# Gated output weights and the context's initial states made during the in-projection and kept in scratch memory

## The chip, the cores and the metric

The kernel runs on one core of one Trainium2 chip. TensorE (PE) multiplies matrices, VectorE (DVE), ScalarE (ACT) and GpSimd (POOL) do the rest, SyncE (SP) issues most transfers. Each engine takes its instructions strictly in the order in which the program lists them. The metric is the device time in microseconds; three runs of the kernel before took 2037.56, 2040.84 and 2042.3 us, median 2040.84.

## The reference

One block of a network over 2048 tokens of width 1024 and 256 context tokens: normalise and modulate, project (`w_in`), mix the tokens by windowed attention and by a gated linear recurrence (mLSTM) run in both directions, project with `w_out`, then 16 experts of which each takes 256 tokens. What bears on the change, cut from the reference:

```
hx = modulate(rmsnorm(x, norm1_w), sh1, sc1);  hc = the same of ctx
aq, ak, av, mq, mk, mv, mo, gates = mixer_inputs(hx, ...)       # and of hc
att  = latent_attention(rope(aq), rope(ak), av, cak, cav, sink)
# DEPTH is 1, so the context only gives the recurrence its two initial states:
st_f = mlstm_state_update(zero, cmk, cmv, cli_f, clf_f)          # C = sum_s ws[s] k[s] v[s]
st_b = mlstm_state_update(zero, flip(cmk), flip(cmv), ...)
h_sum, _, _ = bidir_mlstm(mq, mk, mv, li_f, lf_f, li_b, lf_b, st_f, st_b)   # 16 chunks of 128, each way
mix  = concat([att, rmsnorm_per_head(h_sum) * norm_w * sigmoid(mo)])
x    = x + g1 * (mix @ w_out)                                    # g1: 1024 gates, the same for all tokens
x    = x + g2 * expert_choice_ffn(modulate(rmsnorm(x, norm2_w), sh2, sc2), ...)
```

All is float32. The kernel multiplies float32 matrices by splitting each operand into a rounded part (`hi`) and the rest (`lo`) and adding the products hi*hi, lo*hi and hi*lo.

## The kernel before, in words

**The planner.** Work is written as generators that yield what they need: an engine and a cost (`A(n)` ACT, `V(n)` DVE, `G(n)` POOL, `"P"` PE, `Q(n)` transfers), a token of a buffer pool, or an event. `Flow.run` (L108 on) plays these against a list of clocks, takes on each engine the ready task with the lowest priority number, and so fixes the order of instructions on each engine when the program is built. On the chip that order is kept, and an instruction waits for its operands and for the memory that it overwrites. `Flow(AHEAD)` lets the transfer queue of a phase begin AHEAD us before the phase's other engines.

**phase_in** (L427). `main` (L781) runs over four blocks of 512 tokens and, within a block, over eleven groups of columns of `w_in` (the last ones `mk`, `mv`, `mo`); the products land in the two PSUM buffers `mm`. `conv_out` (L835) empties those of `mq` and `mk` into a buffer `cu` (4 of them), convolves, and stores to `s_mq`, `s_mk`, `s_cmk`; `mo_out` (L906) stores `s_mo`. Attention runs beside it: scores (L258, L262), softmax, transposes of the probabilities (L303), values (L331, L332). `load_x` brings tokens through the buffers `xt` (3) and `hxv` (2). `mod_rest` (L1094) uses the same `xt` for the rest of the modulation weights, in 64 pieces multiplied and added on DVE into `macc`; it writes the gates g1 to `s_row`. `gates` (L1185) makes the recurrence's decay weights in block 3, among them `cws`, the context's.

**phase_mix** (L1365) has 32 visits, alternately the next chunk of the forward and of the backward direction. A visit loads query and key (`raw`, L1650) and value (`vraw`, L1664), makes the weights `wh`, `wl` (`prep_s`, `prep_w`) and the decayed query (`prep_q`, `decb`), gives its output with L1912 and updates the state `C` with L1624; the split state is `cs`. The second visit of a chunk adds both directions, normalises and, in `out_proj` (L2075), multiplies by `w_out` rows 512 to 1023 (weights 4 to 7) and makes router logits. `att_loads`, `att_projs` (L2008, L2034) multiply the attention's part by weights 0 to 3, one chunk after another beside the first visits; the second visits' loads wait until these are done.

The parts that the change touches: `inits` (L1520) loads the context's `cmv` and `cmk`, splits the values into `vsl` (2 buffers), transposes the keys, scales them by `cws` and makes both initial states and their splits. `wouts` and `wout` (L1469, L1498) load g1 and `w_out`, multiply (L1503; L1506 also by the norm's weights), and split into `wo_hi` and `wo_lo` (four pairs, of 128 by 1024; weights 4 to 7 take the same four pairs after the last attention projection). `prep_k` waits for `got_ev`, which `inits` fires late. The first loads' buffers (`raw`, `vraw`, `decb`, `xl`, `hx2t`) lie in one pool on the right side of the memory, where phase_in has `hxp`:

Of the kernel before, what the change touches and what calls it, by code (L numbers as in the profile page):

```python
# [16 lines left out]
try:  # L17
# [15 lines left out]
D = 1024  # L33
# [18 lines left out]
PRI = dict(loadx=1, mod1=0, hx=10, w=5, main=11, sc=6, tr=6, val=8, modr=11, gates=1, norm=6, rows=0, hxsp=3, hx0=1, wsp=0, conv=6, kv=7, q=6, mv=5, mo=5, rq=8, rk=3, value=1, ml=4, mrl=8, sm=10, usp=11, st=11)  # L52
# [3 lines left out]
AHEAD = 5.0  # L56
RIGHT = ("raw", "vraw", "decb", "xl", "hx2t")
# [5 lines left out]
PR = dict(vs=12, masks=7, init=0, load=8, vload=13, wout=6, dir=10, wr=2, hload=11, xload=0, pw=6, pq=5, ps=2, ks=7, se=10, h=2, he=7, xe=2, sc=12, ce=10, wout2=1, pk=13, asp=7, ae=10, ap=13, fi=4, op=13, aload=13, lo=13, af=6)  # L63
# [19 lines left out]
    "row": (2, 1024),  # L83
}
# [23 lines left out]
class Flow:  # L108
# [37 lines left out]
    def follow(self):  # L146
        self.cur.ready -= self.lag["D"]

# [208 lines left out]
class Kernel:  # L357
# [69 lines left out]
    def phase_in(self):  # L427
        nc, tc = self.nc, self.tc
        with ExitStack() as st:
# [26 lines left out]
            self.mod_ev, self.opened, self.main_done, self.rest_ev, self.turned = (Event() for _ in range(5))  # L456
# [21 lines left out]
            fl.spawn(self.gates(), PRI["gates"])  # L478
            fl.run()
# [6 lines left out]
    def load_x(self, units):  # L486
        nc, a, p, tok = self.nc, self.a, self.hxp, self.tok
        for n, u in enumerate(units):
# [4 lines left out]
            for t in range(2):  # L493
                if n < 2:
                    yield self.wm_ev[XW_AT[n]]
                if n < 2:
                    x = (self.ep if n else self.mp).tile([128, D], F32, name=f"xe{t}")
                else:
                    yield tok["xt"]
                    x = self.buf(p, "xt", [128, D])  # L500
# [10 lines left out]
    def norm_x(self, x, ev):  # L511
        nc, p, tok = self.nc, self.hxp, self.tok
        yield tok["hxv"]
        junk = self.buf(p, "hxv", [128, D], BF)
# [391 lines left out]
    def mo_out(self, ps, i, u, t):  # L906
# [17 lines left out]
        (nc.scalar if u == ("x", 7) else nc.sync).dma_start(self.s["mo"][r0:r0 + 128, i * 256:(i + 1) * 256], e)  # L924
# [260 lines left out]
    def gates(self):  # L1185
# [36 lines left out]
        for ct in range(2):  # L1222
# [13 lines left out]
            self.fl.give(mm)  # L1236
        yield mm
# [113 lines left out]

    def logsig_flow(self, x):
# [12 lines left out]
    def phase_mix(self):  # L1365
        nc, tc, a, s = self.nc, self.tc, self.a, self.s
        self.rk = self.last.enter_context(tc.tile_pool(name="rkeep", bufs=1, reuse_waits="tile"))
        with ExitStack() as st:
# [5 lines left out]
            right = pool("pmixr", 1, side="right", reuse_waits="tile")  # L1374
            self.alt = dict.fromkeys(RIGHT, right)
            fl = self.fl = Flow(AHEAD)
            self.bufs = MBUFS
            self.tok = {n: Tokens(k, -AHEAD if n in RIGHT else 0.0) for n, k in MBUFS.items()}
# [5 lines left out]
            self.wo_ev, self.stored, self.wr_ev, self.init_ev = evs(8), evs(NT), Event(), evs(2)  # L1384
            self.got_ev = Event()
            self.mask_ev, self.att_ev, self.wf_ev = Event(), Event(), evs(2)
# [53 lines left out]
    def wrouter(self):  # L1440
        nc, a, one, tok = self.nc, self.a, self.one_p, self.tok
        self.wr = one.tile([128, KT, NE], F32, name="wr")
        yield Q(128)
# [25 lines left out]
    def wouts(self):  # L1469
        nc, a, s, tok, fl = self.nc, self.a, self.s, self.tok, self.fl  # L1470
        yield tok["hx2t"]
        g1b = self.buf(self.pin, "hx2t", [128, 1024])
        yield Q(1024)
        nc.sync.dma_start(g1b, self.dram(s["row"], 0, [[0, 128], [1, 1024]]))
        left = [8]
        for k in range(4):
            yield tok["xl"]
            wf = self.buf(self.pin, "xl", [128, 1024])
            if k == 3:
                fl.fire(self.wf_ev[0])  # L1480
            yield Q(1024)
            nc.sync.dma_start(wf[0:64, :], a["w_out"][k * 64:(k + 1) * 64, :])
            nc.sync.dma_start(wf[64:128, :], a["w_out"][256 + k * 64:256 + (k + 1) * 64, :])
            fl.spawn(self.wout(k, wf, g1b, "xl", left), PR["wout"])
        yield self.s_ev[NT // 2]
        for k in range(4, 8):
            buf = "xn" if k < 6 else "xl"
            if k == 6:
                yield self.am_ev[NT - 1]
            yield tok[buf]  # L1490
            wf = self.buf(self.pin, buf, [128, 1024])
            if k == 7:
                fl.fire(self.wf_ev[1])
# [1331 lines left out]
```

## Time and profile before

| What | Value |
|---|---|
| median of three runs | 2040.84 us |
| the profiled execution | 2042.06 us, of which the span of the trace is 2040.3 |
| busy over the span | PE 1863.0 us (91%), DVE 1595.5 (78%), ACT 1280.7 (63%), POOL 839.1 (41%) |
| instructions | 37000 |
| read and written in HBM | 270.73 MB and 84.54 MB, 174 GB/s over the span |
| mean granted TensorE clock | 0.959 of full speed |

All later numbers of the trace are microseconds from the span's start. "Busy" adds the durations of an engine's instructions; an engine may be busy all the time and still not decide the end, since others may wait for something else. DMA share is the mean busy share of the 16 DMA engines. "[idle before <-X]" behind an instruction says how long its engine stood before it and what ended that.

### The profile page before, as it was taken

The numbers are of one execution on the slowest core, as the hardware profiler recorded it, in microseconds if no ns is written. First come the engines' busy times: TensorE is split into PE (matmuls) and PEld (weight loads), VectorE is DVE, ScalarE is ACT, GpSimd is POOL, SyncE is SP. The second block draws the span as 40 slices with busy tenths as digits, with TensorE's granted clock in tenths as the row PEclk, the third lists the DMA queues.
The fourth block names the chain that finished last, engine by engine and source line by source line (L and its number), as shares of the span: only waits on it lengthen the run. The fifth ranks groups of instructions, "written<-read, shape, count | busy, mean of one in ns | idle before, by whom it ended". The sixth has DMA issues, their size and how long they took to land.

```text
span 2040.3 us, 37000 instructions
## 1 busy us (share of the span) xinstructions
PE 1863.0 (91%) x12921; PEld 1665.6 (82%) x12921; DVE 1595.5 (78%) x3486; ACT 1280.7 (63%) x3144; POOL 839.1 (41%) x820
## 2 busy tenths in 40 slices
PE   7799999999999999996989989994589999999997
PEld 2698998899889989985767767783589999999996
DVE  3799779998998699868999677756667878787772
ACT  4477777787787777775665578865344545454542
POOL 0324234333543243316777665510334535353432
PEclk9899999999999999996999989996699999999999
DMA  8343264345342333227777867646467878888772
GB/s 281 98 145 102 73 189 123 109 149 160 99 120 79 95 84 97 79 82 205 270 255 260 286 224 242 225 145 222 133 203 210 261 226 253 240 235 254 223 233 42
DMA packets 293499, 357.82 MB, mean 175 GB/s; under 512 B 27288, under 2 KB 225592, under 8 KB 292416
## 3 DMA queue, kind: packets, MB, share of 16 engines
q1 hardware_dynamic: 283072, 320.32, 49.9%
q0 software_dynamic: 9376, 34.08, 7.2%
q8 instruction: 102, 1.67, 0.3%
q10 hardware_dynamic: 864, 1.05, 0.1%
q14 instruction: 85, 0.70, 0.1%
HBM read 270.73 MB, written 84.54 MB: 174 GB/s over the span
## 4 chain that ended last, share of the span: by engine, by line
PE 56%; DVE 24%; ACT 8%; DMA 6%; issue 5%; SPq 1%; POOL 0%; POOLq 0%; DVEq 0%; ACTq 0%
PE gu L2684 17%; PE mm L758 9%; PE yp L2736 8%; PE po L2004 5%; DVE w_lo L741 3%; PE t L303 2%; DMA w_raw<-in_w_in 2%; PE s L258 2%; PE o L593 1%; PE t L2628 1%; PE h L1912 1%; PE o L332 1%; PE o L331 1%; PE mm L776 1%; DVE s L280 1%
## 5 line engine op out<-in xcount | busy, mean ns | idle before, releaser
L2529 ACT ACTIVATE ew_hi<-ew_raw 128x1024 fp32r<-128x1024 f32 x184 | 193.6, 1056 | 163.6 <-PE yp L2736 91.5
L2457 DVE TENSOR_TENSOR ew_lo<-ew_raw,ew_hi 128x1024 fp32r<-128x1024 f32 x152 | 215.6, 1428 | 42.0 <-ACT ew_hi L2529 21.4
L291 POOL TENSOR_SCALAR P<-P,am 128x640 f32<-128x640 f32 (+1 forms) x128 | 113.1, 885 | 257.7 <-DVE am L289 145.4
L741 DVE TENSOR_TENSOR w_lo<-w_raw,w_hi 128x256 fp32r<-128x256 f32 (+1 forms) x352 | 157.3, 471 | 30.2 <-ACT w_hi L735 28.1
L2756 POOL DMA_INDIRECT out_x<-y,idx x32 | 57.1, 1786 | 260.7 <-DVE y L2750 175.0
L2684 PE MATMUL gu<-xg_hi,ew_hi 128*128 128x256 f32 x1024 | 148.6, 283 | 0.6 <-DVE xg_hi L2656 0.6
L758 PE MATMUL mm<-w_hi,hx_hi 128*128 128x256 f32 (+1 forms) x944 | 142.5, 288 | 5.2 <-ACT hxr L933 2.2
L735 ACT ACTIVATE w_hi<-w_raw 128x256 fp32r<-128x256 f32 (+1 forms) x352 | 135.2, 410 | 18.9 <-DMA w_raw<-in_w_in 18.1
L758 PE MATMUL mm<-w_hi,hx_lo 128*128 128x256 f32 (+1 forms) x944 | 141.9, 288 | 0.0
L2684 PE MATMUL gu<-xg_lo,ew_hi 128*128 128x256 f32 x1024 | 141.7, 280 | 0.0
L758 PE MATMUL mm<-w_lo,hx_hi 128*128 128x256 f32 (+1 forms) x944 | 141.5, 286 | 0.0
L2684 PE MATMUL gu<-xg_hi,ew_lo 128*128 128x256 f32 x1024 | 141.2, 280 | 0.0
L758 PEld LDWEIGHTS mm<-w_hi,hx_hi 128*128 128x128 f32 x944 | 124.8, 190 | 9.4 <-issue 2.7
L2684 PEld LDWEIGHTS gu<-xg_hi,ew_hi 128*128 128x128 f32 x1024 | 131.2, 189 | 1.0 <-DVE xg_hi L2656 0.9
L2684 PEld LDWEIGHTS gu<-xg_lo,ew_hi 128*128 128x128 f32 x1024 | 129.2, 189 | 0.0
L2684 PEld LDWEIGHTS gu<-xg_hi,ew_lo 128*128 128x128 f32 x1024 | 128.8, 189 | 0.0
L758 PEld LDWEIGHTS mm<-w_hi,hx_lo 128*128 128x128 f32 x944 | 125.0, 191 | 3.3 <-issue 2.6
L758 PEld LDWEIGHTS mm<-w_lo,hx_hi 128*128 128x128 f32 x944 | 124.6, 189 | 1.8 <-issue 0.9
L314 DVE TENSOR_TENSOR pl<-t,ph 128x512 fp32r<-128x512 f32 x156 | 105.8, 684 | 24.4 <-ACT ph L312 23.1
L282 ACT ACTIVATE P<-s,am 128x640 f32<-128x640 f32 (+1 forms) x128 | 99.8, 780 | 31.1 <-DVE am L280 25.7
L2750 DVE SCALAR_TENSOR_TENSOR y<-yp,gv,g2b 128x512 f32<-128x512 f32 x64 | 48.1, 751 | 90.2 <-PE yp L2736 90.2
L280 DVE CUSTOM_DVE_ANT_0 s<-s,mrow,nsink 128x640 f32<-128x640 f32 (+1 forms) x120 | 105.3, 877 | 13.1 <-PE s L262 7.5
(482 smaller groups left out, 5616.4 us busy)
## 6 DMA issues: line engine op xcount, KB each, us to landing
w_raw<-in_w_in SPq DMA_DIRECT2D x176, 256.0 KB
ew_raw<-in_w_gate SPq DMA_DIRECT2D x32, 1024.0 KB
ew_raw<-in_w_up SPq DMA_DIRECT2D x32, 1024.0 KB
ew_raw<-in_w_down SPq DMA_DIRECT2D x32, 1024.0 KB
xt<-in_w_mod SPq DMA_DIRECT2D x64, 256.0 KB
out_x<-xl SPq DMA_DIRECT2D x32, 512.0 KB
s_vs<-vsl SPq DMA_DIRECT2D x16, 516.0 KB
vsl<-s_vs SPq DMA_DIRECT2D x16, 516.0 KB
```

Source lines behind the costliest of these rows:

```text
L280: nc.vector.tensor_tensor_reduce(x, x, mask, 1.0, k.nsink[:, h:h + 1], op0=OP.add, op1=OP.min, accum_out=m[:, 0:1])
L282: nc.scalar.activation(P[:, :n], sc, AF.Exp, bias=m[:, 0:1], scale=-1.0, accum_out=m[:, 1:2])
L291: nc.gpsimd.tensor_scalar(P[:, :n], P[:, :n], m[:, 4:5], 0.0, op0=OP.mult, op1=OP.add)
L314: nc.vector.tensor_sub(lo, pt, f(hi))
L735: nc.scalar.activation(hi, raw[:, k:k + 2, :n], AF.Copy)
L741: nc.vector.tensor_sub(lo, raw[:, k:k + 2, :n], f(hi))
L758: self.nc.tensor.matmul(ps[:, :2 * n].rearrange("p (a b) -> p a b", a=2), lhsT=hx[:, k, t * 128:(t + 1) * 128], rhs=w[:, sl:sl + 2, k, :n] ...
L2004: self.nc.tensor.matmul(po, lhsT=m[:, k, :], rhs=self.wo[k0 + k][wi][:, sl], start=(j == 0), stop=(j == 11))
L2457: (self.nc.vector if eng == "D" else self.nc.gpsimd).tensor_sub(out, x, y)
L2529: nc.scalar.activation(hi[:, sl], raw[:, sl], AF.Copy)
L2684: nc.tensor.matmul(po[:, ft, :], lhsT=w[:, k, ft * 128:(ft + 1) * 128], rhs=x[:, k, :], start=(j == 0), stop=(j == 23))
L2736: nc.tensor.matmul(po[hf], lhsT=hs[i][h][:, ft, t * 128:(t + 1) * 128], rhs=wd[i][w][:, ft, hf * 512:(hf + 1) * 512], start=(j[hf] == 0), ...
```

## The change

- A new task `ahead` in phase_in starts when `mod_rest` is done, with priority 5 (the main chain has 11, scores 6, softmax 10). It loads half of g1 and then half rows of `w_out` into `hxv`, one after another; `wo_split` multiplies them by the gates on DVE, splits them into an `xt` buffer on ACT and POOL and stores both parts to the new scratch `s_wo`. After the gates' weights `cws` it loads `cmv` and `cmk`, makes both initial states as `inits` did, holding all four `cu` buffers meanwhile, and stores them and their splits to `s_C` and `s_cs`.
- In phase_mix `wouts` loads `s_wo` straight into `wo_hi`, `wo_lo` (hi parts first), and `inits` loads `s_cs` and `s_C`; no engine works on them. `wout` is gone, with `got_ev`, for which `prep_k` waited.
- `raw`, `vraw` and `decb` get a pool of their own, taken before the rest of the right side, so that they lie on other memory of phase_in than before; AHEAD is 8 instead of 5.
- The first output weights are loaded behind the first visits' loads (`first_ev`); attention's, the router's and the states' loads and the stores of split values come behind the hi parts (`xs_ev`). The projections wait for each weight as they come to it (`wh_ev`, `wo_ev`) instead of for all four first.
- `masks` gets priority -1 (7 before), and the stores of `mo` of units 6 and 7 are issued by ACT (before: of unit 7; the others by SP).

The diff, cut to its core:

```diff
-AHEAD = 5.0
-RIGHT = ("raw", "vraw", "decb", "xl", "hx2t")
+AHEAD = 8.0
+EARLY, RIGHT = ("raw", "vraw", "decb"), ("xl", "hx2t")
 SCRATCH = {
...
+    "wo": (2, 8, 128, 1024),
+    "C": (2, 128, 516),
+    "cs": (2, 128, 1032),
 def mo_out
-        (nc.scalar if u == ("x", 7) else nc.sync).dma_start(self.s["mo"]...
+        (nc.scalar if u[1] > 5 else nc.sync).dma_start(self.s["mo"]...
+    def ahead(self):
+        yield self.rest_ev
+        for hf in range(2):
+            g1 = p.tile([128, 512], F32, name="macc", bufs=1)
+            yield Q(512)
+            nc.sync.dma_start(g1, self.dram(s["row"], hf * 512, [[0, 128], [1, 512]]))
+            for k in range(8):
+                yield tok["hxv"]
+                wf = self.buf(p, "hxv", [128, 512])
+                yield Q(512)
...
+                ev = Event()
+                fl.spawn(self.wo_split(k, hf, wf, g1, ev), PRI["ahead"])
+                yield ev
+        yield self.cws_ev
...
+        for _ in range(4):
+            yield tok["cu"]
+        Cs = []
+        for d in range(2):
+            ks = []
+            for c in range(2):
+                kf = p.tile([128, 4, 128], F32, name="macc", bufs=1)
+                yield G(512)
+                nc.gpsimd.tensor_mul(kf, kk[:, c], self.cws[:, d, c, :, None].to_broadcast([128, 4, 128]))
+                kh, kl = (self.buf(self.pin, "cu", [128, 4, 128], F32R) for _ in range(2))
+                yield A(512)
+                nc.scalar.activation(kh, kf, AF.Copy)
+                yield V(512)
+                nc.vector.tensor_sub(kl, kf, f(kh))
+                ks += [(kh, vs[c]), (kl, vs[c])]
+            yield tok["hxv"]
+            C = self.buf(p, "hxv", [128, 4, 129])
+            for h in range(4):
+                yield tok["tr"]
+                po = self.buf(self.ps, "tr", [128, 258])
+                yield "P", 0.46
+                for j, (k, v) in enumerate(ks):
+                    nc.tensor.matmul(po, lhsT=k[:, h, :], rhs=v[:, h, :], start=(j == 0), stop=(j == 3))
...
+        for n in ("cu",) * 4 + ("xt",) * 3:
+            fl.give(tok[n])
...
+    def wo_split(self, k, hf, wf, g1, ev):
+        fl.later(3.0)
+        yield V(512)
+        if k < 4:
+            nc.vector.tensor_mul(wf, wf, g1)
...
+        yield tok["xt"]
+        w = self.buf(p, "xt", [128, 2, 512], F32R)
+        yield A(512)
+        nc.scalar.activation(w[:, 0, :], wf, AF.Copy)
+        yield G(512)
+        nc.gpsimd.tensor_sub(w[:, 1, :], wf, f(w)[:, 0, :])
+        fl.give(tok["hxv"])
+        fl.fire(ev)
+        yield Q(1024)
+        nc.sync.dma_start(s["wo"][:, k, :, sl].rearrange("j p n -> p j n"), f(w))
+        fl.give(tok["xt"])
 def wouts
+        for g in range(2):
+            yield self.att_ev if g else self.first_ev
+            ks = range(4 * g, 4 * g + 4)
+            self.wo[4 * g:4 * g + 4] = [tuple(one.tile([128, 1024], F32R, name=f"wo_{n}{k}") for n in ("hi", "lo")) for k in range(4)]
+            for i, evs in enumerate((self.wh_ev, self.wo_ev)):
+                for k in ks:
+                    yield Q(1024)
+                    nc.sync.dma_start(f(self.wo[k][i]), s["wo"][i, k])
...
 def inits
+        yield self.xs_ev
+        for d in range(2):
+            if d:
+                yield self.lo_ev
+            self.cs[d] = p.tile([128, 4, 129], F32, name=f"C{d}"), p.tile([128, 4, 258], F32R, name=f"cs{d}", bufs=1)
+            yield Q(1032)
+            nc.sync.dma_start(f(self.cs[d][1]), s["cs"][d].rearrange("p (h v) -> p h v", h=4))
...
 def preps
             if v["ct"] < NT - 1:
-                yield self.got_ev
                 yield tok["ks"]
 def proj
                 if k % 2 == 0:
+                    for ev in (self.wo_ev if wi else self.wh_ev)[k0 + k:k0 + k + 2]:
+                        yield ev
                     yield "P", 0.435
 def x_loads
-        yield self.wf_ev[1]
+        yield self.am_ev[NT - 1]
```

## Rows read from the trace of the kernel before

**Rows 1.** Windows: length; busy us (count) of PE, PEld, DVE, ACT, POOL; clock; DMA share; GB/s.

```profile
522.00:911.00 389.00, 376.40 (x2883) 353.41 (x2881) 333.61 (x908) 301.51 (x800) 139.51 (x197) 1.00 0.32 90
911.00:956.00 45.00, 24.16 (x100) 17.09 (x99) 35.25 (x44) 21.62 (x45) 22.97 (x17) 0.62 0.71 199
956.00:1120.00 164.00, 148.22 (x811) 116.87 (x811) 156.87 (x295) 100.28 (x258) 127.69 (x102) 0.97 0.80 264
1120.00:1169.00 49.00, 47.97 (x237) 37.91 (x235) 33.55 (x66) 23.85 (x74) 31.61 (x29) 1.00 0.87 285
1169.00:1180.00 11.00, 3.00 (x13) 1.93 (x14) 11.00 (x9) 4.65 (x13) 10.68 (x5) 0.62 0.28 89
1180.00:1400.00 220.00, 206.59 (x1177) 168.35 (x1176) 144.36 (x403) 171.92 (x555) 89.11 (x87) 0.95 0.62 209
```

**Rows 2.** Timeline of PE at the seam: start, us, line, operation, tiles, count, idle before.

```profile
910.63 0.43 PE L332 MATMUL o<-pl,cvt 128*128 128x512 f32 x1
...
955.95 0.39 PE L1912 MATMUL h<-vsl,wh 128*128 128x258 f32 x1
956.17 0.28 PE L1912 MATMUL h<-vsl,wl 128*128 128x258 f32 x1
956.29 0.28 PE L1912 MATMUL h<-cs,qh 128*128 128x258 f32 x1
```

**Rows 3.** Timeline of SP's issues at the seam.

```profile
897.45 7.59 SPq L924 DMA_DIRECT2D s_mo<-moe  x2
...
910.12 0.37 SPq L1532 DMA_DIRECT2D raw<-s_cmk  x1
...
912.84 0.59 SPq L1650 DMA_DIRECT2D raw<-s_mq  x1
...
943.85 0.50 SPq L1664 DMA_DIRECT2D vraw<-s_mv  x1
```

**Rows 4.** Groups by line and form, DVE, 911 to 956: count, busy us, mean ns, idle before.

```profile
L1503 DVE TENSOR_TENSOR xl<-xl,hx2t 128x1024 f32<-128x1024 f32 x4 | 9.0, 2301 | 0.0
L1603 DVE TENSOR_TENSOR ks_l<-tmp,ks_h 128x512 fp32r<-128x512 f32 x5 | 5.5, 1103 | 1.2 <-ACT ks_h L1596 1.1
L1603 DVE TENSOR_TENSOR tmp<-raw,cws 128x512 f32<-128x512 f32 x4 | 4.1, 1028 | 0.1
L1603 DVE TENSOR_TENSOR wo_lo<-xl,wo_hi 128x1024 fp32r<-128x1024 f32 x2 | 3.2, 1582 | 0.0
L1563 DVE TENSOR_TENSOR C<-C,h 128x258 f32<-128x258 f32 x4 | 1.7, 416 | 2.1 <-ACT C L1561 2.1
```

**Rows 5.** Timelines of POOL, DVE and ACT at the seam: visit 0's preparation.

```profile
907.66 0.76 POOL L1420 DMA_DIRECT2D nm<-s_nm  x1 [2.99 <-PE mm L758]
...
920.48 0.69 DVE L1725 TENSOR_TENSOR decb<-raw,t 128x512 f32<-128x512 f32 x1 [4.19 <-DMA raw<-s_mq]
...
929.57 0.63 ACT L1596 ACTIVATE wh<-e 128x512 fp32r<-128x512 f32 x1
...
930.28 1.27 POOL L1603 TENSOR_TENSOR wl<-e,wh 128x512 fp32r<-128x512 f32 x1 [0.74 <-ACT wh L1596]
```

**Rows 6.** Timelines of POOL, DVE and PE around 1172: weights 4 to 7 are split.

```profile
1171.40 3.32 POOL L1603 TENSOR_TENSOR wo_lo<-xn,wo_hi 128x1024 fp32r<-128x1024 f32 x1
...
1172.44 3.37 DVE L1603 TENSOR_TENSOR wo_lo<-xl,wo_hi 128x1024 fp32r<-128x1024 f32 x1
...
1179.54 0.58 PE L1624 MATMUL h<-vsl,ks_h 128*128 128x258 f32 x1 [5.35 <-DVE hh L1899]
```

**Rows 7.** Windows of the in-projection.

```profile
540.00:620.00 80.00, 74.08 (x580) 70.28 (x580) 78.00 (x191) 66.91 (x171) 37.30 (x45) 1.00 0.41 119
620.00:740.00 120.00, 117.40 (x902) 110.85 (x901) 92.65 (x267) 90.70 (x257) 39.46 (x58) 1.00 0.32 88
740.00:820.00 80.00, 76.86 (x598) 71.38 (x597) 76.90 (x217) 62.52 (x156) 26.93 (x42) 1.00 0.32 92
```

**Rows 8.** Timeline of ACT: the last convolution buffer is filled.

```profile
813.02 0.59 ACT L857 ACTIVATE cu<-mm 128x512 f32<-128x512 f32 x1
```

More of the change, by code (lines that the diff above doesn't have):

```diff
@@ L51 @@
 X_AT = (("mq", 0), ("mk", 1))
-PRI = dict(loadx=1, mod1=0, hx=10, w=5, main=11, sc=6, tr=6, val=8, modr=11, gates=1, norm=6, rows=0, hxsp=3, hx0=1, wsp=0, conv=6, kv=7, q=6, mv=5, mo=5, rq=8, rk=3, value=1, ml=4, mrl=8, sm=10, usp=11, st=11)
+PRI = dict(ahead=5, loadx=1, mod1=0, hx=10, w=5, main=11, sc=6, tr=6, val=8, modr=11, gates=1, norm=6, rows=0, hxsp=3, hx0=1, wsp=0, conv=6, kv=7, q=6, mv=5, mo=5, rq=8, rk=3, value=1, ml=4, mrl=8, sm=10, usp=11, st=11)
 BUFS = dict(t=2, mm=2, s=1, tr=1, o=1, xt=3, hxv=2, w_raw=3, cu=4, cv=2, vs=1, moe=3, hxr2=4, hxr4=5, hr=1, ropet=3, ropew=2, ropeu=1, q2t=4, gate=8, gatet=2, am=6, P=8, ph=2, pl=2)
@@ L1520, in inits @@
-    def inits(self):
-        nc, p, s, fl, tok = self.nc, self.pin, self.s, self.fl, self.tok
-        items = []
-        for c in range(2):
-            yield tok["vraw"]
-            vr = self.buf(p, "vraw", [128, 4, 129])
+        nc, s, one, fl = self.nc, self.s, self.one_p, self.fl
+        for g in range(2):
[6 more added lines that the diff above has]
+                    nc.sync.dma_start(f(self.wo[k][i]), s["wo"][i, k])
+                    fl.spawn(self.there(evs[k]), 0)
+                    fl.issued()
+                if not g:
+                    fl.fire(self.lo_ev if i else self.xs_ev)
@@ new lines, in there @@
+    def there(self, ev):
+        yield "Q", 0.0
+        self.fl.fire(ev)
+    def inits(self):
+        nc, p, s, fl = self.nc, self.pin, self.s, self.fl
+        yield self.xs_ev
+        for d in range(2):
+            if d:
+                yield self.lo_ev
+            self.cs[d] = p.tile([128, 4, 129], F32, name=f"C{d}"), p.tile([128, 4, 258], F32R, name=f"cs{d}", bufs=1)
+            yield Q(1032)
+            nc.sync.dma_start(f(self.cs[d][1]), s["cs"][d].rearrange("p (h v) -> p h v", h=4))
+            fl.spawn(self.there(self.init_ev[d]), 0)
+            fl.issued()
+        for d in range(2):
@@ L1569, in inits @@
-        for n in ("raw", "raw", "vsl", "vsl"):
-            fl.give(tok[n])
     def split_state(self, d, C):
@@ L2035, in att_projs @@
         nc, a, fl, tok = self.nc, self.a, self.fl, self.tok
-        for k in range(4):
-            yield self.wo_ev[k]
         for c, ev in zip(ORDER, self.am_ev):
@@ L2076, in out_proj @@
         nc, p, fl, tok, v = self.nc, self.pin, self.fl, self.tok, self.v[i]
-        for k in range(4, 8):
-            yield self.wo_ev[k]
         ss = self.sm.tile([128, 1], F32, name="xss")
```

186 lines of the change are left out of this document (85 added, 101 removed).

## The prediction

> **What bounds the kernel now.** I read the share of busy time by stage first, then the instructions in order of time around the seam between in-projection and mixing phase, then SP's issues, then what DVE did there, then the busy time of the in-projection's stretches. [rows 1] cut the span at 522 us (mod_rest ends there, so the new work can start), 911 (the in-projection's last matmul), 956 (first visit), 1120, 1169 (attention projections done), 1180 and 1400. From 522 to 911 PE is busy 376.4 of 389 us at full clock: PE bounds it. From 911 to 956 it is busy 24.2 of 45 us at a granted clock of 0.62. From 956 to 1120 DVE bounds (156.9 of 164, DMA share 0.80). From 1169 to 1180 PE is again nearly still (3.0 of 11) and DVE is full. Then PE bounds until 1400; the experts behind it are untouched.
>
> The seam: the last attention matmul starts at 910.63, the first of visit 0's output matmuls (L1912) at 955.95 [rows 2], 45 us later. Two things fill these 45 us. The loads come late: SP stands 7.6 us at the s_mo stores, gets the buffer for the context's keys at 910.12, issues visit 0's query load at 912.84 and the second value load at 943.85 [rows 3]. And engines split things that do not depend on the visits: of DVE's 35.25 busy us, output weights (L1503, wo_lo) and the context's states (ks_l, tmp, C) take most [rows 4].
>
> **Part A, the seam.** Before: 45 us from the last in-projection matmul to visit 0. After, from three sides.
> Chain: nm is issued at 907.66, before the end, since only its memory was awaited; dec follows on the same queue, so both are there by about 912 (an estimate: some 4 us after the issue, half of the 7.6 that the query load took among other loads). With query and key loaded before, visit 0 needs what it needed here from the query's landing (DVE starts decb at 920.48) to the end of wl (930.28+1.27=931.55): 11.1 us [rows 5]. First visit at 912+11=923: 33 us earlier. State 0, loaded behind 2.1 MB of weights at 264 GB/s (8 us), keeps up with that.
> DVE: removed are the four multiplies (9.0), two wo_lo (3.2), four of five ks_l (4.4), the tmp (4.1) and the C (1.7) [rows 4]: 22.4 of 35.25 us. The rest, 12.9, and the 9.75 us in which DVE idled make 22.6, so the state of 956 is reached 22 us earlier.
> DMA: 45 us at 199 GB/s [rows 1] are 9.0 MB. Out go 3.1 MB (raw output weights 2.1, gate row 0.5, context 0.5); 1.6 MB (visits 0 and 1) move ahead of the seam; in come 5.8 MB (weights hi and lo 4.2, states 1.6). 10.1 MB at the next stage's 264 GB/s are 38 us: only 7 us earlier.
> I take the DVE figure, -22 us: the stage that follows is full on DVE and not on DMA [rows 1]. Ends kept: -33 and -7. What is late next is visit 2, whose loads queue behind the 4.2 MB.
>
> **Part B, the second half of the weights.** At 1169 the splits of weights 4 to 7 hold DVE: wo_lo takes 3.37 us from 1172.44 while POOL has one from 1171.40, and PE stands until 1179.54 for hh, queued behind them on DVE [rows 6]. PE's 8.0 idle us of 11 [rows 1] go at most. In their place 4.2 MB instead of 2.1 must be loaded, and only when the attention projections have freed the tiles: at the 285 GB/s of the stage from 1120 to 1169 [rows 1] 14.7 us, in which visits run but no output projection, and the loads queued behind on SP's queue wait. If PE stood all of it, the cost would be 14.7-8.0=+7. I take -2 (visits fill about 9 of the 14.7), ends -8 and +7.
>
> **Part C, the in-projection.** Added, at the durations of [rows 2, 5]: on PE 8 transposes and 32 matmuls, 40 steps of 0.12 us (956.17 to 956.29): 4.8 us. On DVE 16 multiplies and 4 subtractions at 0.69 and ten small ones, together about 17 us. On ACT about 27 copies, 0.63 us or less each: some 15. On POOL 24 operations at 1.27: 30.5 us. On SP some 50 issues, among them 16 stores that wait for POOL's subtraction and stand ahead of later w_raw loads. The mo stores of unit 6 move from SP to ACT, four issues, beside PE's tail.
> PE's 4.8 us have no cover: PE is 97% busy. DVE has 55 us free over the whole stretch, but where? Idle 2.0 us of 80 from 540 to 620, 27 of 120 from 620 to 740, 3.1 of 80 from 740 to 820 [rows 7]. The weights (from 522, one half row after another) fall largely into the first full stretch, the states (they need the gates' weights, made in block 3) into the second. By that some 14 of the 17 us meet a full DVE; PE idles 5.9 and 3.1 us in these stretches now [rows 7], so PE follows DVE there in part, and I charge half: 7. ACT (301.5 of 389) has room. The states also take all four cu buffers, which the convolutions need: the last is emptied into cu at 813 [rows 8]. C: +12, ends +4.8 (PE alone) and +37 (PE, all of DVE's 17, half of POOL's 30.5).
> The VectorE-GpSimd port bears on that upper end. In the row wo_lo ends at 1175.81, 1.09 us after POOL's ended at 1174.72, though they began 1.04 us apart [rows 6]: it was held until POOL was done. The Trainium skill, "SBUF — State Buffer", section "Who interferes with whom", says that an instruction of VectorE with two SBUF inputs and one of GpSimd that reads SBUF exclude one another, the later one waiting for the whole of the other. The trace agrees; by that rule alone every subtraction moved to POOL can hold a full DVE, and the sum would be rival 3's.
>
> **Sum.** The profiled execution took 2042.06 us (span 2040.3 and 1.76 around it). -22 -2 +12 = -12: 2030.1. The median of the three runs, 2040.84, lies 1.2 under the profiled one: **2029 us**.
>
> **Rivals.** All are set against 2042.06 and lowered by the same 1.2.
> 1. The in-projection hides all but PE's work, and visit 0's chain is the limit: -33 -2 +4.8 = -30, 2011 us. For it: DVE idles 55 us before 911. Against: not where the new work falls.
> 2. Front bound by DMA: -7 -2 +12 = +3, 2044 us, no change. For it: 0.80 to 0.87 DMA share from 956 to 1169 and 4.2 MB net more in this phase (10.0 in, 5.8 out). Against: with 20% of the DMA engines' time unused, DVE was full.
> 3. The other side, slower: the in-projection pays more than the seam returns. One mechanism: the new task is served ahead of attention and of the main chain, so where DVE is full its multiplies, and POOL's subtractions that hold DVE, push softmax and evacuations back one for one, and while it holds the four cu buffers (four rounds of 1.27+0.63+0.69, some 10 us, and the evacuations of eight sums) the last convolutions keep both mm buffers and PE's main chain stands. -22 -2 +37 = +13, 2054 us. It decides from 24 us of growth of the in-projection on; by +28 the result is clearly slower. Against: 27 us of DVE room right behind the first full stretch.
> 4. The change doesn't do what it says: the early loads find SP or their memory taken and come after the seam again; then the query lands as late as here, 8 us (912.84 to 920.48 [rows 3, 5]), A is -14 and the time 2037 us.
>
> **Chances.** Forecast 0.42, rival 1 0.16, rival 2 0.18, rival 3 0.19, rival 4 0.05. A change under 0.2% (4 us) can't be told from none here. Faster: 0.40 of the forecast, 0.16, 0.06 of rival 2, 0.02 of rival 4: 0.64. Same: 0.02, 0.10, 0.03 of rival 3, 0.03 of rival 4: 0.18. Slower: 0.02 of rival 2 and 0.16 of rival 3: 0.18. The forecast's own range is 2018 to 2038; with the other cases, leaving out half of rival 1's lower side and rival 3 beyond +12, 2008 to 2052.
>
> **What would show it.** A: from the last L332 to the first visit output 12 to 28 us instead of 45, DVE without L1503 between them, raw<-s_mq issued before the last L332. B: no wo_lo on DVE or POOL in the mixing phase, a PE gap after the attention projections that ends on a DMA of wo_hi or wo_lo. C: the last L332 between 916 and 935, with more PE idle than now in 540 to 620 and 740 to 820. The forecast is wrong if the last L332 lies beyond 939 (rival 3), if first visits wait for raw or cs loads (rival 2), or if the stage up to 1169 isn't shorter although the seam is.

## The result, and the profile after

The changed kernel took 2055.6 us (median of 4 runs, 2054.34 to 2056.79) beside 2041.57 of the kernel before in the same comparison: ratio 1.0072, 95% interval 1.0054 to 1.0089. It is slower by 14 us where 12 us faster were forecast; the profiled span went from 2040.3 to 2055.0.

Three instants cut that difference: the last matmul of the in-projection (before it is attention's, L332; now it is the main chain's, L765), the first output matmul of visit 0 (L1912, now L1978), the last output projection (L2004, now L2072: the start of its last matmul, 1391.4 before and 1405.9 after). The main chain itself ends at 933.8 instead of 909.8, attention (now L338) at 921.3 instead of 910.6.

| us, profiled executions | before | after | difference | forecast |
|---|---|---|---|---|
| last matmul of the in-projection | 910.6 | 933.8 | +23.2 (C) | +12 |
| from there to visit 0 (the seam) | 45.3 | 24.6 | -20.7 (A) | -22 |
| visit 0 to the last output projection | 435.5 | 447.5 | +12.0 (B) | -2 |
| from there to the end | 648.9 | 649.1 | +0.2 | 0 |

The windows of the changed kernel at the cuts of [rows 1], with the in-projection's whole new length ahead of them (columns as there):

```profile
522.00:934.00 412.00, 385.96 (x2913) 358.48 (x2911) 364.52 (x935) 316.14 (x828) 168.70 (x221) 1.00 0.43 127
911.00:956.00 45.00, 37.74 (x227) 31.58 (x226) 21.47 (x42) 27.99 (x65) 10.46 (x13) 0.83 0.67 223
956.00:1120.00 164.00, 144.71 (x793) 114.53 (x793) 150.06 (x291) 97.42 (x256) 126.01 (x102) 0.94 0.82 270
1120.00:1169.00 49.00, 49.00 (x235) 39.46 (x234) 25.87 (x46) 17.18 (x47) 27.20 (x25) 1.00 0.77 261
1169.00:1180.00 11.00, 8.57 (x40) 6.22 (x38) 8.00 (x19) 8.59 (x31) 6.72 (x6) 0.84 0.77 291
1180.00:1400.00 220.00, 201.91 (x1117) 163.57 (x1118) 137.16 (x379) 168.11 (x549) 89.45 (x88) 0.94 0.63 212
```

PE's idle time in the in-projection went from 12.6 (389.0-376.4) to 26.0 us and its busy time up by 9.6, which together make the 23; DVE's busy time went up by 31 us where 17 were counted. At 1169 the gap is gone, as forecast (PE 8.6 of 11 instead of 3.0), but from 1180 to 1400 PE ran 60 matmuls fewer.

The seam, timeline of PE (as [rows 2]):

```profile
933.00 1.12 PE L765 MATMUL mm<-w_lo,hx_hi 128*128 128x256 f32 x8
937.38 0.62 PE L1805 MATMUL t<-dec,sel 64*128 64x512 f32 x1 [3.27 <-ACT moe L928]
...
958.40 0.28 PE L1978 MATMUL h<-vsl,wh 128*128 128x258 f32 x1
```

SP's issues (as [rows 3]); the first two lie before the end of the in-projection now:

```profile
916.03 0.37 SPq L1713 DMA_DIRECT2D raw<-s_mq  x1
...
931.10 1.76 SPq L1727 DMA_DIRECT2D vraw<-s_mv  x2
935.76 1.96 SPq L1609 DMA_DIRECT2D wo_hi<-s_wo  x4
```

DVE from 934 to 959 by line and form (as [rows 4]): no weight, no context state, only the visits' own work:

```profile
L1666 DVE TENSOR_TENSOR vsl<-vraw,vsl 128x516 fp32r<-128x516 f32 x2 | 2.4, 1198 | 0.0
L1666 DVE TENSOR_TENSOR xn<-raw,xn 128x512 fp32r<-128x512 f32 x2 | 2.2, 1120 | 0.7 <-ACT xn L1659 0.7
```

The in-projection's stretches (as [rows 7]): PE does less in each of the three, and DVE fills the room it had from 620 to 740:

```profile
540.00:620.00 80.00, 69.44 (x532) 65.56 (x531) 75.62 (x171) 61.16 (x153) 36.54 (x45) 0.98 0.55 165
620.00:740.00 120.00, 115.51 (x860) 106.29 (x858) 108.59 (x284) 96.08 (x264) 55.44 (x69) 1.00 0.51 151
740.00:820.00 80.00, 74.34 (x580) 69.06 (x580) 76.53 (x201) 61.10 (x154) 33.01 (x43) 1.00 0.35 97
```

What follows 820 shows most. The main chain's matmuls have two lines: most groups of columns use L758 (after: L765), the groups that go to a convolution, mk and mq, use L776 (after: L783). The windows of the first line alone (length, PE busy, clock, DMA share, GB/s), first of the kernel before, then of the changed one:

```profile
820.00:847.00 27.00, 14.67 (x112) 1.00 0.32 88
```

```profile
820.00:847.00 27.00, 0.00 (x0) 1.00 0.17 48
```

That line alone doesn't show that the chain stands: L776 ran none here, L783 ran 53 in the changed kernel, which was at this instant still in its convolution groups. But those end early. In the changed kernel's timeline of PE these two are neighbours on the main chain, whichever line one takes:

```profile
832.88 1.10 PE L783 MATMUL mm<-hx_hi,w_lo 128*128 128x256 f32 x8
...
854.11 0.72 PE L765 MATMUL mm<-w_hi,hx_hi 128*128 128x256 f32 x4
```

And ACT's timeline in the changed kernel. The states' first splits fill cu buffers at 810; the last two convolutions are emptied into theirs at 851, where [rows 8] had 813:

```profile
810.54 0.64 ACT L1427 ACTIVATE cu<-macc 128x512 fp32r<-128x512 f32 x1
...
851.15 1.09 ACT L864 ACTIVATE cu<-mm 128x512 f32<-128x512 f32 x2
```

For 20.1 us, from 834.0 to 854.1, the main chain doesn't run: both mm buffers hold sums that wait for cu, and it goes on 3 us after the first begins to be emptied. In the kernel before no gap of the chain between 790 and 870 is longer than 3.5 us. PE does attention meanwhile and looks busy; the lack shows as a longer tail, in which the main chain ends 12.5 us behind attention.

### The profile page after: what moved, and what is told of

Its sections match the earlier page's. It is cut to its first block, busy times and chain, and to the rows that moved or that the text cites. A ratio compares the mean times of both kernels' runs of the same rounds, so it can differ in the third digit from the quotient of the medians.

```text
span 2055.0 us, 37148 instructions
## 1 busy us (share of the span) xinstructions
PE 1875.0 (91%) x12921; PEld 1671.7 (81%) x12921; DVE 1584.3 (77%) x3485; ACT 1285.2 (63%) x3157; POOL 842.9 (41%) x836
## 4 chain that ended last, share of the span: by engine, by line
PE 38%; DVE 8%; ACT 4%; DMA 3%; issue 3%; POOL 2%; SPq 0%; POOLq 0%; DVEq 0%; ACTq 0%
PE gu L2749 17%; PE yp L2801 8%; PE po L2072 4%; PE mm L765 2%; PE t L2693 1%; PE h L1978 1%; PE t L2196 1%; ACT ho L2007 1%; PE t L1805 1%; POOL cs L1666 1%; PE t L309 0%; ACT ho L2024 0%; DVE C L2285 0%; PE h L1687 0%; DMA out_x<-xl 0%
## 5 line engine op out<-in xcount | busy, mean ns | idle before, releaser
L765 PE MATMUL mm<-w_hi,hx_hi 128*128 128x256 f32 (+1 forms) x944 | 143.0, 288 | 6.2 <-ACT hxr L940 2.2
L765 PE MATMUL mm<-w_hi,hx_lo 128*128 128x256 f32 (+1 forms) x944 | 141.7, 288 | 0.0
L765 PE MATMUL mm<-w_lo,hx_hi 128*128 128x256 f32 (+1 forms) x944 | 141.3, 287 | 0.0
L765 PEld LDWEIGHTS mm<-w_hi,hx_hi 128*128 128x128 f32 x944 | 125.1, 190 | 10.1 <-ACT hxr L940 2.6
L765 PEld LDWEIGHTS mm<-w_hi,hx_lo 128*128 128x128 f32 x944 | 124.9, 190 | 3.8 <-issue 2.8
L765 PEld LDWEIGHTS mm<-w_lo,hx_hi 128*128 128x128 f32 x944 | 124.9, 190 | 1.2 <-issue 0.4
L320 DVE TENSOR_TENSOR pl<-t,ph 128x512 fp32r<-128x512 f32 x156 | 105.0, 682 | 13.1 <-ACT ph L318 11.7
```

Of the source, the lines that this page charges most:

```text
L320: nc.vector.tensor_sub(lo, pt, f(hi))
L765: self.nc.tensor.matmul(ps[:, :2 * n].rearrange("p (a b) -> p a b", a=2), lhsT=hx[:, k, t * 128:(t + 1) * 128], rhs=w[:, sl:sl + 2, k, :n] ...
```

## The experiments

Ratios are to the kernel before, measured beside each, with 95% intervals. The stages are cut as above, from one profiled execution each. Repeated runs of one kernel differ by up to 12 us, so differences of a few us between two profiles mean little; the medians carry the verdicts. Every edit also changes what the planner reckons with, so the order of instructions can change with it: an edit's effect is that of its work and of the order that comes with it.

| run | ratio (interval) | median us | last in-projection matmul | seam | mix |
|---|---|---|---|---|---|
| changed kernel | 1.0072 (1.0054, 1.0089) | 2055.6 | 933.8 | 24.6 | 447.5 |
| E1 no engine work ahead | 0.9987 (0.9971, 1.0004) | 2038.5 | 915.4 | 23.1 | 445.6 |
| E2 weights' work out | 1.0034 (1.0021, 1.0047) | 2047.9 | 928.4 | 21.8 | 445.9 |
| E2b states' work out | 1.0003 (0.9989, 1.0017) | 2040.6 | 918.4 | 22.3 | 446.5 |
| E3 no GpSimd subtractions | 1.0064 (1.0039, 1.0089) | 2055.6 | 933.3 | 22.7 | 446.8 |
| E4 half the bytes | 1.0009 (0.9995, 1.0023) | 2042.6 | 933.4 | 22.7 | 434.9 |
| E5 ACT's queue | 1.0071 (1.0048, 1.0093) | 2055.0 | 931.7 | 22.2 | 445.4 |
| E6 states late | 1.0042 (1.0026, 1.0058) | 2050.8 | 930.4 | 21.5 | 448.9 |
| E7 second half in the mix | 1.0077 (1.0048, 1.0105) | 2055.4 | 938.4 | 22.4 | 436.1 |
| E8 = E6 and E7 | 0.9995 (0.9985, 1.0005) | 2040.9 | 933.7 | 21.2 | 438.6 |
| E9 low priority | 1.0203 (1.0184, 1.0221) | 2083.2 | 943.9 | 39.7 | 449.5 |
| E10 = E8, weights late | 1.0029 (1.0017, 1.0041) | 2045.8 | 930.3 | 21.3 | 440.0 |
| E11 states in the mix | 1.0053 (1.0035, 1.0071) | 2053.8 | 922.0 | 37.6 | 445.6 |
| E12 = E8, t buffers | 1.0003 (0.9991, 1.0016) | 2042.0 | 928.4 | 21.2 | 442.4 |
| E13 = E8, one product | 0.9998 (0.9985, 1.0010) | 2040.6 | 929.7 | 21.2 | 438.5 |
| E14 early loads alone | 1.0005 (0.9994, 1.0017) | 2041.6 | 911.2 | 45.3 | 436.7 |
| E15 = E10, states later | 1.0007 (0.9996, 1.0018) | 2041.3 | 926.4 | 21.2 | 440.7 |
| E16 = E8, states later | 0.9975 (0.9963, 0.9987) | 2034.8 | 922.1 | 21.3 | 442.3 |

**Whose work stretches the in-projection.** E1, E2 (its first two lines) and E2b:

```
 wo_split:  - multiply, ACT copy, GpSimd subtraction, one store of [128, 2, 512]
            + for j in range(2): nc.sync.dma_start(s["wo"][j, k, :, sl], wf)
 ahead:     - splits, transposes, sums and splits of the states (from "kk" on)
            + stores of vrs[d] to s["C"][d] and, twice, to s["cs"][d]
```

> Leaves out all engine work of the new task in the in-projection (multiplies, splits, states); its loads and stores stay and the scratch gets the raw data, so the mixing phase does the same work as in the changed kernel. Theory: the 24 us by which the in-projection grew (last matmul 933.8 instead of 909.8) are its engines' work; then it ends at 910 to 916 and the time is 2055.6-24 = 2032 (2028 to 2038), the 13 us lost after the attention projections staying. Rival: buffers shared with the x tiles, SP's issues and the stores stretch it; then the last matmul stays beyond 925 and the time at or above 2045.

> Leaves out the multiplies and splits of the output weights in the in-projection (loads and stores stay, the scratch gets raw weights); the context's states are made as in the changed kernel. Theory (each engine instruction displaces where the engine is full, the weights have 16 of the new DVE multiplies and 16 of the 24 GpSimd operations): about 14 of the 24 us go, 2055.6-14 = 2042 (2038 to 2046). Rival (the four cu buffers held by the states from 803 to 850 stop the convolutions): at most 5 us go, 2051 or more.

> Leaves out the engine work of the context's states in the in-projection (raw context values are stored in their place), the weights are made as in the changed kernel. Theory (the two parts add up: without weights 2047.9, without both 2038.5, so the states are 9.5 us): 2046 (2043 to 2049), the last matmul of the in-projection at 918 to 924, with main-chain matmuls between 820 and 848. Rival (each part alone fills the free room, only the two together cost): 2040 or less.

The end moved from 933.8 to 915.4 without both, 928.4 without the weights' work, 918.4 without the states'. So by this instant the states' work costs 13.0 to 15.4 us, the weights' 3.0 to 5.4, and the loads and stores the remaining 4.8; by the medians it is 9.4 to 15.0 for the states and 2.1 to 7.7 for the weights. The two ways of taking one out give different figures, and the difference is as large as the weights' price. PE's idle time says where: from 522 to 740 it is 8.9 us before, 15.3 in the changed kernel, 7.8 in E2 and 14.8 in E2b, so that the weights' work sits there; from 740 to 860 it is 3.6, 10.3, 11.2 and 3.8, so that the states' sits there. E1's stage came out as expected and its time 0.5 us above its range; E2b's stage too, its time 2.4 us below its range; E2 lies between its two theories. In E2b the main chain runs on (no gap above 5.3 us from 790 to 870, and L765 has in the window from 820 on):

```profile
820.00:847.00 27.00, 14.00 (x104) 1.00 0.29 86
```

**The subtractions on GpSimd.** E3 drops the 16 of the weights:

```
-        nc.gpsimd.tensor_sub(w[:, 1, :], wf, f(w)[:, 0, :])
-        nc.sync.dma_start(s["wo"][:, k, :, sl].rearrange("j p n -> p j n"), f(w))
+        for j in range(2):
+            nc.sync.dma_start(s["wo"][j, k, :, sl], f(w)[:, 0, :])
```

> Leaves out GpSimd's 16 subtractions of the output weights in the in-projection (the high part is stored in both places); everything else is as in the changed kernel. Theory (a GpSimd subtraction holds a full DVE, that is why PE idles 15.3 us from 522 to 740 instead of 8.9): idle 9 to 12 us there and 2050 to 2053. Rival (the multiplies on DVE and their place before softmax are the cost, GpSimd works beside): idle 14 us or more and 2054 to 2057.

DVE's multiplies by line and form (count, busy us, mean ns, idle before), changed kernel, then E3, both from 522 to 740:

```profile
L1469 DVE SCALAR_TENSOR_TENSOR hxv<-hxv,cols,macc 128x512 f32<-128x512 f32 x8 | 7.7, 960 | 0.0
L1467 DVE TENSOR_TENSOR hxv<-hxv,macc 128x512 f32<-128x512 f32 x8 | 5.8, 723 | 0.0
```

```profile
L1469 DVE SCALAR_TENSOR_TENSOR hxv<-hxv,cols,macc 128x512 f32<-128x512 f32 x8 | 7.1, 882 | 0.0
L1467 DVE TENSOR_TENSOR hxv<-hxv,macc 128x512 f32<-128x512 f32 x8 | 5.5, 683 | 0.0
```

More than these new multiplies, old ones took longer at the same count: the sums of the rotary embedding. Kernel before, changed kernel, E3:

```profile
L964 DVE TENSOR_TENSOR hxr<-hxr,ropeu 128x128 f32<-128x128 f32 x10 | 3.5, 351 | 0.7 <-POOL hxr L961 0.6
L971 DVE TENSOR_TENSOR hxr<-hxr,ropeu 128x128 f32<-128x128 f32 x10 | 8.5, 848 | 0.7 <-POOL hxr L968 0.6
L971 DVE TENSOR_TENSOR hxr<-hxr,ropeu 128x128 f32<-128x128 f32 x10 | 3.3, 331 | 0.0
```

Idle time of PE from 522 to 740 fell from 15.3 to 11.6 us, as the theory has it, but from 740 to 860 it rose from 10.3 to 12.6, and the time did not move. The holding of DVE is there (848 against 331 ns, 723 against 683) and was not the price: without the subtractions DVE is busy 8.3 us less from 522 to 860, and PE's idle time there is 24.2 us, 25.6 in the changed kernel.

**The bytes behind the attention projections.** E4 loads half; E5 loads all on another queue:

```
 E4:  + if g and i: self.wo[k] = (self.wo[k][0],) * 2   (no load of wo_lo 4..7)
 E5:  - nc.sync.dma_start(...)   + (nc.scalar if g else nc.sync).dma_start(...)
```

> Of the second half of the output weights only the high parts are loaded (2.1 MB instead of 4.2), the projection reads them in place of the low parts. Theory (after the attention projections the visits' loads stand behind 4.2 MB on SP's queue, that is the 13 us lost there): half of the 15 us of transfer goes, 2055.6-7.5 = 2048 (2045 to 2051). Rival (the order of the work and the clock changed, the bytes don't matter): 2054 to 2057.

> The eight loads of the second half of the output weights are issued on ACT's queue instead of SP's. Theory (the visits' loads wait because they stand behind the weights on one queue): visits go on beside the transfer and 4 to 9 us of the 13 come back, 2047 to 2052. Rival (the memory's bandwidth is what is short, or ACT is held by the issues): no gain, 2054 to 2060.

Stretch from 1180 to 1214, columns as in [rows 1]: kernel before, changed kernel, E4, E5.

```profile
1180.00:1214.00 34.00, 33.20 (x169) 26.20 (x169) 24.30 (x61) 28.61 (x99) 21.84 (x19) 0.92 0.78 261
```

```profile
1180.00:1214.00 34.00, 29.88 (x132) 24.10 (x133) 13.40 (x43) 19.75 (x60) 8.48 (x8) 0.80 0.83 295
```

```profile
1180.00:1214.00 34.00, 31.88 (x162) 24.78 (x163) 23.23 (x60) 27.38 (x92) 17.91 (x16) 0.90 0.69 240
```

```profile
1180.00:1214.00 34.00, 29.81 (x138) 23.45 (x139) 12.06 (x41) 20.55 (x59) 9.18 (x9) 0.85 0.75 274
```

In the changed kernel DVE has 13 us of work in 34, where it had 24, and PE, at a granted clock of 0.80 instead of 0.92, ran 132 matmuls instead of 169. SP's issues and PE's visit outputs there:

```profile
1170.99 1.87 SPq L1609 DMA_DIRECT2D wo_hi<-s_wo  x4
1172.95 2.39 SPq L1609 DMA_DIRECT2D wo_lo<-s_wo  x4
1175.50 0.55 SPq L1713 DMA_DIRECT2D raw<-s_S  x1
```

```profile
1178.92 0.42 PE L1978 MATMUL h<-cs,ql 128*128 128x258 f32 x1
...
1203.22 6.52 PE L2196 MATMUL t<-wr,hx2t 128*128 128x16 f32 x32 [1.34 <-ACT hx2t L2189]
...
1210.33 0.56 PE L1978 MATMUL h<-vsl,wh 128*128 128x258 f32 x1
```

For 31 us no visit has an output. Loads behind the 4.2 MB may account for the time up to about 1200, but not for the rest: the weights wl of the next visit are done at 1199.4 and its values were asked for at 1197.0, while PE first goes through output projections of two chunks and the router's 32 matmuls.

E4 took back 12.6 us of the mix (447.5 to 434.9), more than the 7.5 expected, and its time lies below the theory's range: with 2.1 MB the stage is as before. So the theory had the place right and the size too small. But the planner counts transfers, so E4 has another order of PE's work as well as fewer bytes. E5 took back at most 2 us of the mix and nothing of the time, as its rival has it. It doesn't show why, since the queue changes and PE's order hardly does. E5's visit load and next visit output (its profiled run is its fastest, 2052.2):

```profile
1167.18 0.43 SPq L1713 DMA_DIRECT2D raw<-s_S  x1
1207.14 0.56 PE L1978 MATMUL h<-vsl,wh 128*128 128x258 f32 x1
```

The load was issued 8.3 us sooner, and PE had the same output projections and router matmuls to go through first; it also stood 3.2 us for wo_hi. So neither the transfer nor the order is ruled out as the limit.

**Two repairs.** E6 waits before taking cu; E7 gives the second half back to the mix; E8 has both:

```
 E6:  + yield self.reach[3, ("mv", 0)]          (ahead, before the four tok["cu"])
 E7:  + if k > 3: store the scaled wf once, return        (wo_split)
      + k 4..7: load into xn/xl before att_ev, split behind it   (wouts, as before)
```

> The states' task takes the four cu buffers only once the main chain has begun its last value groups, behind the last convolution; everything else is as in the changed kernel. Theory (the states cost 13 us because they hold the cu buffers from 803 to 850, the last convolutions keep both mm buffers and no main-chain matmul runs from 820 to 848): the main chain runs on, only PE's 4.8 us of the states stay, the last matmul of the in-projection comes 6 to 9 us earlier, time 2046 to 2050. Rival (the states' own work on full engines displaces other work wherever it stands): no gain, 2053 to 2058.

> Weights 4 to 7 are only multiplied in the in-projection and stored once; the mixing phase loads 2.1 MB of them before the attention projections end and splits them behind, as the kernel before did. Theory (the 12 us lost behind the attention projections are the 4.2 MB that could be loaded only then): mix 435 instead of 447.5 us, and 1 to 2 us less in the in-projection, time 2040 to 2044. Rival (the splits on DVE there are as dear as the transfer): 2050 or more.

> The edits of the two runs before together. Theory (two independent losses): 2055.6-13-7 = 2035 (2031 to 2040), faster than the kernel before. Rival (the visits that come earlier meet another limit in the mixing phase): 2041 or more.

E6's expectation, that no main-chain matmul runs from 820 to 848, counted one of the chain's two lines; it stood from 834 to 854. In E6 no gap of the chain is above 5.3 us there, yet it gained only 3.4 us in the in-projection and 5 in the median, less than its theory: the buffers are a part, not the whole. E7's mix fell to 436.1 as forecast, but its in-projection got 4.6 us longer and the time did not change; its four runs lie between 2048.4 and 2060.0, and the profiled one is the fastest, 7 us under the median. The reordered in-projection stalled elsewhere, and that was not followed; the chain's gap is still 19.9 us. Together they reach the kernel before, not the 2035 expected. E6 alone gave 4.8 us, E7 alone 0.2, both 14.7: the two losses are not independent, as E8's theory had them.

**When the work ahead is served.** E9 changes a number (`ahead=5` to `ahead=12`), E10 starts the weights at `self.reach[2, ("mv", 0)]`:

> The new task's priority in the in-projection goes from 5 to 12, behind the main chain and the attention; nothing else changes. Theory (the weights' 5 us come from DVE instructions of the task that stand ahead of softmax where DVE is full): 2 to 5 us less, 2050 to 2054. Rival (the order doesn't matter, the work itself does, or the states now come too late): 2054 to 2062.

> As the run with both edits (2040.9), and the output weights are made only from the third block's value groups on, about 615 us, where DVE idled 27 us of 120 before. Theory (work placed where DVE is full costs, where it idles it doesn't): PE's idle time from 522 to 620 falls from 10.2 to about 6.3, time 2036 (2033 to 2039). Rival (the work costs as much in the later stretch, or arrives late): 2040 or more.

E9 lost 28 us more, in its rival's direction and far beyond its range: the states' sums are still being made at 930 to 950, s_C and s_cs are stored at 954, and visit 0 starts at 983.6. In E10 idle time from 522 to 620 fell to 6.5 us, as expected, and came back from 740 to 860 (9.4), where the delayed weights now met the states: its rival holds. (E10's profiled execution was its fastest run, 2041.7.)

**One part alone.** E11 makes the states in the mix as before, beside the weights ahead; E14 is the kernel before with the early loads, their own buffers and the mo stores on ACT, and nothing ahead.

```
 E11: ahead without its states; inits as in the kernel before; weights late as in E10,
      weights 4 to 7 split in the mix as in E7, weights 0 to 3 loaded behind self.ld[1]
 E14: + EARLY pool for raw, vraw, decb; AHEAD = 8.0; masks first; mo stores of u[1] > 5 on ACT;
      inits takes both vsl and both raw buffers before its first load
```

> Only the output weights are made in the in-projection (from about 615 us on, the second half of them split in the mixing phase); the context's states are made in the mixing phase as the kernel before did, beside the early loads of the first visits. Theory (the states cost more in the in-projection than in the seam, where DVE idled 9.75 us): last matmul of the in-projection at 914 to 919, seam 28 to 35 us, mix 436, time 2034 (2029 to 2040). Rival (with the states the seam is full again): seam 40 us or more, 2044 or more.

> The kernel before with the early loads alone: their own buffers, the gate's stores of units 6 and 7 on ACT's queue, masks first; weights and states are made in the mixing phase as before. Theory (the seam is bound by DVE's splits and by the chain of the states): seam 38 to 45 us, time 2036 to 2042. Rival (the loads were what the seam waited for): seam 25 to 33 us, 2024 to 2032.

E14's query load is issued at 908.31, before the last attention matmul, and still the seam is 45.3 us (SP, then PE):

```profile
908.31 0.57 SPq L1650 DMA_DIRECT2D raw<-s_mq  x1
```

```profile
911.16 0.42 PE L332 MATMUL o<-pl,cvt 128*128 128x512 f32 x1
...
956.47 0.39 PE L1912 MATMUL h<-vsl,wh 128*128 128x258 f32 x1
```

So the loads alone gain nothing. E11 puts a number on the states in the seam: 37.6 against 21.3 us in E10, for 8.3 us less in the in-projection; since E10's profile is of its fastest run and E11's of its slowest (2057.9), part of the 16.3 may be the spread of runs. With a mix of 445.6 its 2053.8 is far from the 2034 expected, and nearer to its rival.

**What of the states costs.** E12 takes their sums to the t buffers, E13 leaves three of four products out:

```
 E12: - self.buf(self.ps, "tr", ...)   + self.buf(self.ps, "t", ...)
 E13: - for j, (k, v) in enumerate(ks): matmul(..., start=(j == 0), stop=(j == 3))
      + matmul(po, lhsT=ks[0][0][:, h, :], rhs=ks[0][1][:, h, :], start=True, stop=True)
```

> As the run with both edits (states late, second half of the weights split in the mixing phase; 2040.9), and the states' transposes and sums go through the two t buffers of PSUM instead of the single tr buffer that attention's query transposes need. Theory (the sums, each emptied by ACT and DVE, hold tr and delay the queries and so the scores): 3 to 5 us less, 2036 to 2038. Rival (the t buffers are as busy, or the sums' buffer doesn't matter): 2040 or more.

> As the run with both edits, with one of the four products of each state sum (8 matmuls instead of 32; the other three are left out). Theory (PE is full, its steps have no cover): 24 steps of 0.12 us and what follows on them, 3 to 4 us less, 2037 to 2038. Rival (the states cost by the waits of ACT, DVE and buffers): at most 1 us less, 2040 or more.

Neither moved the median by more than 1.2 us from E8's: the transposing buffer and PE's products carry little of the price, as far as runs that spread by 8 us can tell; the 2.9 us that 24 steps would cost alone can't be told from none here. (E8's profiled execution took 2045.1, 4 above its median, so its 933.7 is high; E12 and E13 show 928.4 and 929.7.)

**Where DVE has room.** E15 and E16 add one wait to E10 and E8, ahead of the states' first load:

```
         yield self.cws_ev
+        yield self.reach[3, ("mv", 1)]
         vrs = []
```

> As the run with everything late (2045.8), with the whole making of the states moved behind the start of the last value group (about 840 us instead of 780), to where DVE was busy 36 of 51 us before (860 to 911). Theory (the states cost because DVE is full from 740 to 860): PE's idle time there falls from 9.4 to about 5, the last matmul of the in-projection comes at 920 to 925, time 2034 to 2039. Rival (the work costs PE the same wherever it is put in the in-projection, or the states come too late for the first visits): 2041 or more.

> As the run with both edits (2040.9), with the whole making of the states moved behind the start of the last value group; the weights stay early. Theory: idle from 740 to 860 falls from 7.3 to about 4, last matmul 922 to 927, time 2035 to 2039. Rival: 2041 or more.

E16 takes 2034.8 us, 0.25% less than the kernel before (0.13 to 0.37): the only run here that is faster than it clear of the noise, at the lower edge of its theory. Stretch 740 to 860, columns as in [rows 1]: kernel before, changed kernel, E6, E16.

```profile
740.00:860.00 120.00, 116.44 (x888) 108.49 (x887) 110.42 (x308) 90.78 (x227) 39.21 (x61) 1.00 0.31 87
```

```profile
740.00:860.00 120.00, 109.68 (x828) 100.26 (x828) 114.07 (x306) 91.58 (x234) 48.17 (x65) 1.00 0.30 85
```

```profile
740.00:860.00 120.00, 112.03 (x853) 103.27 (x852) 112.31 (x300) 89.74 (x226) 45.39 (x66) 1.00 0.33 90
```

```profile
740.00:860.00 120.00, 117.02 (x897) 108.67 (x896) 106.62 (x298) 87.24 (x221) 41.61 (x65) 1.00 0.35 101
```

PE's idle time: 3.6, 10.3, 8.0, 3.0. In E16 the last convolution is emptied into cu at 821.97 and the states' sums are evacuated between 868 and 894; no gap of the main chain from 790 to 870 is above 5.3 us; the in-projection ends at 922.1, 11.5 us later than before, the seam is 21.3. E15, with the weights late too, keeps 7.5 us idle there and gains nothing over the kernel before: the weights then occupy the room, as far as the profile shows.

## Why the prediction was wrong

**Part A held in its number and in the reason for the old seam.** -20.7 against -22. E14 confirms the reason: with the loads early and the splits left in the seam it stays at 45.3, so the query's landing didn't set it. In the changed kernel, from 933.8 to 958.4, DVE is busy the 12.9 us that were counted:

```profile
933.80:958.40 24.60, 17.34 (x51) 11.24 (x50) 12.90 (x22) 13.12 (x29) 9.99 (x10) 0.65 0.94 334
949.97 0.29 POOL L1565 CAST bones<-ho 128x128 bf16<-128x128 f32 x1 [7.93 <-DMA ho<-in_rconst]
```

But it idles 11.7, so DVE doesn't bound the seam any more: that the whole came out so near is partly luck. POOL stands 7.9 us for a load that is issued behind the first weights, and the DMA share is 0.94; what sets the 24.6 us now was not tested. E11, with the weights gone from the seam and the states left, kept 37.6 of 45.3 us. Rivals 1 and 4 are out. Rival 2's -7 is out by the number; its bound by transfer may well be what is left here (334 GB/s, where it reckoned with 264).

**Part C failed in size: +23.2 instead of +12.** The step that failed is the one that charged half of the DVE time meeting a full DVE, 7 us, for weights and states alike. By E1, E2 and E2b the weights cost 3.0 to 5.4 us at the end of the in-projection, the states 13.0 to 15.4, and the loads and stores, which had no term, 4.8. The states' price is one of place: begun at 780 they take the cu buffers ahead of the last convolutions, the main chain stands for 20.1 us (834.0 to 854.1), and their work falls into the stretch where DVE is full. E6 repairs the buffers alone, which closes the chain's gap, and gets some 5 us; E16 moves all of it behind and gets 4 (by the ratios) to 6 us more (by the medians) against E8, with PE's idle time back at the level of before. The prediction had the cu buffers, but only in rival 3, as an upper end. PE's own 4.8 us, the one term said to have no cover, was not found by itself: E13 removes 24 of its 40 steps and gains 0.3 us, within the spread of its runs, while PE's busy time grew by 9.6 us, which no run takes apart. The mark set for C, the last attention matmul between 916 and 935, was met at 921.3 with the term nearly doubled: it watched attention, while the main chain ended last, at 933.8.

How DVE's room and the cu buffers share the rest is not separated further: E16 relieves both. Of the 31 us by which DVE's busy time grew, against 17 counted, some 19 are the new instructions; some 12 are old ones that took longer, above all the rotary sums beside GpSimd's subtractions (848 instead of 351 ns). E3 shows that this part was no price.

The Trainium skill, "SBUF — State Buffer", section "Who interferes with whom", was weighed for the upper end. The trace agrees with the rule in the durations (848 ns beside the subtractions, 331 without them); the time that it would have cost was not found in E3 (2055.6 us with and without them).

**Part B failed: +12.0 instead of -2, beyond its end of +7.** The failed step is "visits fill about 9 of the 14.7". The visits' loads are issued behind the 4.2 MB, and PE's order puts output projections and the router ahead of the next visit, so visits don't fill the gap, they are in it: 16 visit output matmuls from 1180 to 1214 where there were 48, none for 31 us. That the loss hangs on loading 4.2 MB there, E4 shows by the bytes (mix 434.9) and E7 by the arrangement of before (436.1). Whether it is the transfer or the order fixed with it stays open: both runs change both. The sign set for B, a PE gap that ends on a load of wo_hi or wo_lo, didn't come in the changed kernel. The gap at 1169 [rows 6] did give back 5.6 us of PE's 8.0 idle.

**Rival 3's time (2054) came true, in part for its own reason.** Its mechanism of the cu buffers is what the trace shows in C, but at +23.2, short of the +24 from which it was to decide and far from its +37; its other mechanism, GpSimd's holding of DVE, was no price. The rest of the loss arose in B, where it reckoned with -2 like the forecast. What came, +23, -21 and +12, needs C near twice its central value and B beyond its end together, which the range of the sum left out.

## What to carry to other kernels

Work moved out of a stall is paid where it lands: before pricing its instructions, look which buffers it holds there and whether the engine that it needs is the full one; begun at 780 the same states stretched the in-projection by 13 to 15 us; begun behind the last convolution it ended 4 us later than without them (922.1 in E16 against 918.4 in E2b, where E16 also leaves half of the weights' splits to the mix). Splitting data ahead and reloading it doubles the bytes; where they could only be loaded when a buffer came free, the mix took 447.5 us, with half of them 434.9. A stage filled by PE at 97% can still be stretched by a chain that stands while other matmuls run: count the matmuls of each chain by window, over every line that the chain has, not PE's busy share.

## What was not expected of the hardware

Sixteen subtractions on GpSimd, put beside work of DVE that had not changed, made ten of DVE's sums take 848 ns each instead of 351, and without the subtractions they took 331; still the kernel's time was the same with and without them (2055.6 us). Loading the second half of the weights from ACT's queue instead of SP's let the visits' load be issued 8.3 us sooner (1167.18 instead of 1175.50), and the time stayed at 2055.0 us, with the same work ahead of the visit on PE.
